# Delta rule's opening: constants and a decay exponential made beforehand, three DMA issues moved from ScalarE to SyncE, modulation sums moved to the rotating PSUM banks

## The chip, the cores and the metric

The kernel runs on one core of one Trainium2 chip. A core has five engines that run side by side, each with its own instruction queue worked off in order: TensorE (PE in the profile; its weight loads are shown as PEld), VectorE (DVE), ScalarE (ACT), GpSimd (POOL) and SyncE (SP), which here only issues DMAs. ScalarE can issue DMAs too; such an issue stands in ScalarE's own queue (ACTq), one of SyncE in SPq. TensorE writes its products to PSUM, which has eight banks; VectorE and ScalarE read them from there.

The metric is the device time of one execution in microseconds (us), as the median of several runs.

## The reference

Two layers of a diffusion backbone on 256 latent tokens, with 256 context tokens as a prefix, width 1024, all in float32. Each layer is a mixer, then a SwiGLU, each followed by a layer normalization, with shift, scale and gate ("modulation") that come from a conditioning vector. Layer 0's mixer is attention, layer 1's a chunked gated delta rule. What matters here, cut down:

```python
def reference(...):
    for i in range(DEPTH):
        mod_lat = jnp.split((silu(c) @ w_mod[i] + b_mod[i])[:, None, :], 6, axis=-1)
        u_lat = modulate(h_lat, mod_lat[0], mod_lat[1])        # the context likewise
        y_ctx, y_lat = mla_mixer(...) if i % 2 == 0 else gdn_mixer(...)
        h_lat = layer_norm(ALPHA * h_lat + mod_lat[2] * y_lat, ln1_g[i], ln1_b[i])
        f_lat = swiglu(modulate(h_lat, mod_lat[3], mod_lat[4]), w_ffn_in[i], w_ffn_out[i])
        h_lat = layer_norm(ALPHA * h_lat + mod_lat[5] * f_lat, ln2_g[i], ln2_b[i])

def gdn_project(h, w_in, conv_w, a_log, dt_bias):
    proj = h @ w_in
    qkv = short_conv(proj[..., :GDN_QKV_W], conv_w)            # 5 taps along the tokens, then silu
    q, k, v = ...                                              # q and k normalized per head
    z = proj[..., GDN_QKV_W:GDN_QKV_W + GDN_VW]
    ba = proj[..., GDN_QKV_W + GDN_VW:].reshape(B, T, 2, 2, GDN_V_HEADS)
    beta = sigmoid(ba[..., 0, :])
    g = -exp(a_log) * softplus(ba[..., 1, :] + dt_bias)        # the log decay of each step
    return q, k, v, z, beta, g

# delta rule, in chunks, forward and backward, per head:
# S_t = exp(g_t) (I - beta_t k_t k_t^T) S_{t-1} + beta_t k_t v_t^T,  o_t = S_t^T q_t
```

## The kernel before

Activations lie with the features on the 128 partitions, in eight blocks, and the tokens (256 context, 256 latent) along the free axis. Weights are streamed from HBM in tiles; ScalarE rounds each to a reduced type (`whi`, L185) and VectorE takes the rest (`wlo`, L186), and a product of float32 quality is three matmuls (`mm3`, L213 to L215). The order on each engine is not written out by hand: a planner lays out the instructions by priority, mostly that of the program's order, with a model of their times, so an instruction can stand before or behind others of the program; `after(x)` keeps instructions behind `x` on its engine. Once laid out, each engine works its queue in order.

PSUM is handed out by tags. `bank(name, tag)` takes a bank of the tag given. In layer 0's second half (`psB`) seven banks rotate under the tag `bank` and one stands alone under `md`. In the delta rule (`psC`) the same eight are divided anew: two `pj`, one `tp`, two `inv`, two `ch`, one `av`. A bank of the new division can be written once the last reader of the old tile in it is done.

The modulation is made in chunks (`Chunks`, L309 and on): a chunk `(layer, part)` has eight rows of 512 KB, each four matmuls into one PSUM tile (`modps`, L347; the profile shows two records for each), then a copy by ScalarE (`modsb`, L351), a fold by TensorE (L354) and an addition by VectorE (L356), which ends the use of the bank. `mods_in` says which pool, buffers and PSUM tag the chunks use from there on.

Around the change the program goes thus:

- `swiglu_wide` ends layer 0. Its output blocks (`ffo`) are joined to `h`; each block is squared by ScalarE (L414) for the variance, and the sums go to TensorE (`lnstat`, L424).
- Chunks (1,2) and (1,3) come next, with rows as half tiles `raw` in eleven buffers and with the one `md` bank. `normalize` makes mean and factor (`rs_y`, L244 to L248) and spreads them over a bank each (`lnbc`, L476).
- `make_uh` normalizes `h` (L513, L514), modulates it (`uw`, L517) and splits it into `uhi` (L518) and `ulo` (L519). Behind the last split ScalarE writes the layer's `h` (L522), and its queue issues the store of `h` to DRAM (`hl_dram`, L1470).
- Three `head` products take three banks of `bank` (L1474): the 64 rows for `beta` and `g`, and the first two key blocks.
- `gdn` begins. ScalarE issues the loads of a mask (`cmask`, L839) and of matrices for sums (`gsum`, L860). VectorE makes `cw` (half the taps, L841), `gn` (L843) and `eye` (L846). The first head is copied (L861), turned by TensorE (`batp`, L864), and a chain of small operations makes `beta` and `g` from it (L874 to L916); in it ScalarE makes `al`, the exponential of `a_log` (L893), and VectorE changes its sign (L894).
- Then the steps of `GDN_STEPS`. `keys0` convolves the two key heads (`conv`: a copy with a factor by ScalarE, L943, four taps by VectorE, L946, then tanh, L947, and L949). `queries0`, `values0`, `keys1` and so on project first (`product`) into a bank that `proj_bank` picks, from `pj` and `ch` in turn, and convolve it. `base` makes a decay matrix of a group and eliminates it on GpSimd (L1057, L1058, then L1077 and L1078 in turn); `decays` masks its own on GpSimd (L1134); `invert` uses the eliminated matrices on TensorE (`T`, L1192).

Of the kernel before, what the change touches and what calls it, by code (L numbers as in the profile page):

```python
# [9 lines left out]
F32 = mybir.dt.float32  # L10
F32R = mybir.dt.float32r
I32 = mybir.dt.int32
AF = mybir.ActivationFunctionType
ALU = mybir.AluOpType
AX = mybir.AxisListType.X
PSUM = bass.MemoryType.PSUM

P = 128
D = 1024
NB = D // P  # L20
TS = 256
T = 2 * TS
# [12 lines left out]
def _take(n):  # L35
    global _off
    o = _off
    _off += n
    return o
# [7 lines left out]
PC_CONV = _take(160)  # L47
PC_GN = _take(1)
PC_DT = _take(32)
PC_AL = _take(32)  # L50
# [14 lines left out]
GC_CMASK = _take(64)  # L65
# [31 lines left out]
def tile_trunk(ctx: ExitStack, tc: tile.TileContext, xT, params, consts, gconsts, wmod, w0, w1, out):  # L97
    nc = tc.nc
    V, S, G, PE = nc.vector, nc.scalar, nc.gpsimd, nc.tensor

    cp = ctx.enter_context(tc.tile_pool(name="cp", bufs=1))
# [4 lines left out]
    def open_pool(st, name, bufs=1, **kw):  # L106
        return st.enter_context(tc.tile_pool(name=name, bufs=bufs, reuse_waits="tile", **kw))
# [5 lines left out]
    def bank(name="bank", tag="bank"):  # L113
        tags = env["tags"]
        if tag not in tags:
            tag = next(t for t in ("bank", "ch", "pj") if t in tags)
        return env["ps"].tile([P, 512], F32, name=name, tag=tag, bufs=tags[tag])


    def after(ins):  # L120
        return nullcontext() if ins is None else tc.issue_after(ins.ins)


    par = cp.tile([P, NPAR], F32, name="par")
    nc.scalar.dma_start(out=par, in_=params)
    ident = cp.tile([P, P], F32, name="ident")
# [150 lines left out]
    S.activation(sc, craw, AF.Tanh, scale=0.5)  # L277
    V.scalar_tensor_tensor(sc, sc, 1.0, craw, op0=ALU.add, op1=ALU.mult)
    V.tensor_scalar(cst[:, :, 0:2], sc.rearrange("p (k s) -> p k s", s=2), 0.5, None, op0=ALU.mult)
    modv = [cp.tile([P, 48, 2], F32, name=f"modv{l}") for l in range(2)]  # L280

    def mod_part(l, js, i):
# [77 lines left out]
    def chunks(*lc):  # L360
        return [(l, c, k) for l, c in lc for k in range(8)]

    def mods_in(pool, bufs, bufs2=1, tag="md", rows="mraw"):
        env["mraw"] = (pool, rows, bufs, "modsb", bufs2, tag)

    def flush_mods():
        env["mods"].step(96)


    def mod(l, c):  # L370
        return modv[l][:, 8 * c:8 * c + 8]

    def lnp(l, i):
        o = PC_LN + l * 32 + i * 8
        return par[:, o:o + 8]

    def tok(s):
        return slice(s * TS, s * TS + TS)
# [8 lines left out]
    def ln_mod(l, g, b, lm, c_shift, c_scale):  # L387
        s1 = cp.tile([P, 8, 2], F32, name="ln1s", tag="ln1s")
        A = cp.tile([P, 8, 2], F32, name="lnA", tag="lnA")
        B = cp.tile([P, 8, 2], F32, name="lnB", tag="lnB")  # L390
        V.tensor_scalar(s1, mod(lm, c_scale), 1.0, None, op0=ALU.add)
        V.tensor_tensor(A, s1, lnp(l, g).unsqueeze(2).to_broadcast([P, 8, 2]), op=ALU.mult)
        V.tensor_tensor(B, s1, lnp(l, b).unsqueeze(2).to_broadcast([P, 8, 2]), op=ALU.mult)
        V.tensor_tensor(B, B, mod(lm, c_shift), op=ALU.add)
        return A, B
# [11 lines left out]
    class Residual:  # L407
# [3 lines left out]

        def square(self, m):
            sq = self.pool.tile([P, self.n], F32, name="lnsq", tag="lnsq", bufs=2)
            S.activation(sq, self.r[m], AF.Square)  # L414
            return sq


# [89 lines left out]
    def make_uh(r, mb, rs, ins, A, B, u, streams, pool, l, g, b, hh, sl):  # L507
        done = [ins, ins]
        n = rs.shape[1]
        for fb in range(NB):  # L510
            if mb is not None:
                with after(done[-2]):
                    V.tensor_tensor(r[fb], r[fb], mb, op=ALU.subtract)  # L513
            done.append(V.tensor_tensor(r[fb], r[fb], rs, op=ALU.mult))  # L514
            w = pool.tile([P, n], F32, name="uw", tag="lnsq", bufs=2)
            for i, s in enumerate(streams):
                S.activation(w[:, tok(i)], r[fb][:, tok(i)], AF.Identity, scale=A[:, fb, s:s + 1], bias=B[:, fb, s:s + 1])  # L517
            hi = S.activation(u[0][:, fb, 0:n], w, AF.Copy)  # L518
            last = V.tensor_tensor(u[1][:, fb, 0:n], w, f32(u[0][:, fb, 0:n]), op=ALU.subtract)  # L519
        for fb in range(NB):  # L520
            with after(hi):
                S.activation(hh[fb], r[fb][:, sl], AF.Identity, scale=lnp(l, g)[:, fb:fb + 1], bias=lnp(l, b)[:, fb:fb + 1])  # L522
        return last

    def new_u(shape=(P, NB, T)):
        return (bp.tile(list(shape), F32R, name="uhi", tag="uhi"), bp.tile(list(shape), F32R, name="ulo", tag="ulo"))
# [304 lines left out]
    def gdn(st, u, head, pool, big, fetch_base):  # L831
# [3 lines left out]
        def tl(shape, tag, bufs=1, dt=F32):  # L835
            return pool.tile(list(shape), dt, name=tag, tag=tag, bufs=bufs)

        cmask = tl([P, 2, 32], "cmask")
        nc.scalar.dma_start(out=cmask.rearrange("p d t -> p (d t)"), in_=gconsts[:, GC_CMASK:GC_CMASK + 64])  # L839
        cw = tl([P, 5, 32], "cw")  # L840
        V.tensor_scalar(cw.rearrange("p a b -> p (a b)"), par[:, PC_CONV:PC_CONV + 160], 0.5, None, op0=ALU.mult)  # L841
        gn = tl([P, 1], "gn")
        V.tensor_scalar(gn, par[:, PC_GN:PC_GN + 1], 0.5, None, op0=ALU.mult)  # L843
        XA = [tl([P, 8, 64], f"XA{i}") for i in range(2)]
        eye = tl([P, 32], "eye")
        V.reduce_sum(eye, ident.rearrange("p (b i) -> p i b", b=4), axis=AX)  # L846


        b1, b2, b3 = big(), big(), big()
        gsum, bavt = b1[:, 0:6 * P], b1[:, 6 * P:8 * P]  # L850
        bsb, gT = b2[:, 0:T], b2[:, T:T + P]

        def col(t):
            return t.rearrange("p (d u c e) -> p d u c e", d=2, u=8, c=4)
# [2 lines left out]
        yv, e, s_, q_ = (b3[:, i * 2 * P:i * 2 * P + 2 * P] for i in range(4))  # L857
        s2 = b2[:, T + P:T + 3 * P]
        beta, gcc, ngc, egc, edec, egl, neg = (col(tl([P, P], n)) for n in ("beta", "gcc", "ngc", "egc", "edec", "egl", "neg"))
        nc.scalar.dma_start(out=gsum, in_=gconsts[:, 0:6 * P])  # L860
        S.activation(bsb[0:64], head[0][0:64], AF.Copy)  # L861
        tp = bank("batp", "tp")
        for c in range(4):
# [25 lines left out]
        V.scalar_tensor_tensor(q_, q_, 1.0, s_, op0=ALU.add, op1=ALU.mult)  # L889
        V.tensor_scalar(q_, q_, 2.0, None, op0=ALU.mult)  # L890
        V.scalar_tensor_tensor(q_, yv, 0.0, q_, op0=ALU.max, op1=ALU.add)
        al = b2[:, T + 3 * P:T + 3 * P + 32]
        S.activation(al, par[:, PC_AL:PC_AL + 32], AF.Exp)  # L893
        V.tensor_scalar(al, al, -1.0, None, op0=ALU.mult)  # L894
        for d in range(2):
            V.tensor_tensor(col(e[:, 0:P])[:, d], col(q_[:, 0:P])[:, d], rows(al, d), op=ALU.mult)
        gs = bank("gsums", "inv")
# [473 lines left out]
    i = FFN0_AT  # L1371
# [17 lines left out]
    with tc.tile_pool(name="xin", bufs=1, reuse_waits="tile") as xp:  # L1389
# [4 lines left out]
        for f in range(0, NB, 2):  # L1394
# [3 lines left out]
            for fb in (f, f + 1):  # L1398
                for s in range(2):
                    a, b = A[:, fb, s:s + 1], mod(0, 0)[:, fb, s:s + 1]  # L1400
# [19 lines left out]
    wq = open_pool(l0, "wq", 8)  # L1420
    hp = open_pool(l0, "hp0")
    ln = open_pool(l0, "ln0")
    h = hp.tile([P, NB, T], F32, name="h")
    nc.sync.dma_start(out=h, in_=xT)
    g = gate(0, 2)
    res = Residual(Blocks(rp.tile([P, NB, T], F32, name="r", tag="r")), T, ln, Blocks(h))
    op = parts(o)
    env["ffn"] = dict(wp=wq, raw=11, halves=True)
    for m in range(NB):
        p = bank("mo")  # L1430
# [13 lines left out]
    res = Residual(Blocks(h), T, ln, Blocks(h))  # L1444
# [14 lines left out]
    with tc.tile_pool(name="ffn0", bufs=1, reuse_waits="tile") as pool:  # L1459
        swiglu_wide(st0, ops, res, pool, rp, finish)  # L1460
    flush_mods()
    A, B = ln_mod(0, 2, 3, 1, 0, 1)
    u = new_u()
    mods_in(wq, 5, 1, "md", "raw")
    env["mods"] = Chunks(chunks((1, 2), (1, 3)))
    mb, rs, ins = res.normalize()
    flush_mods()
    hl = dr.tile([P, NB, TS], F32, name="hl_dram")
    make_uh(res.r, mb, rs, ins, A, B, u, (0, 1), ln, 0, 2, 3, Blocks(h[:, :, 0:TS]), tok(1))
    nc.scalar.dma_start(out=hl, in_=h[:, :, 0:TS])  # L1470


    env["wp"], env["ahead"], env["raw"], env["halves"] = wp1[0], 6, 2, False
# [8 lines left out]
    def big():  # L1482
        return np_.tile([P, 1024], F32, name="N", tag="N", bufs=NBUF)

    def latent():
        return Blocks(*(big().rearrange("p (m t) -> p m t", m=4) for _ in range(2)))
# [6 lines left out]
    with tc.tile_pool(name="gdn", bufs=1, reuse_waits="tile") as pool:  # L1493
        last = gdn(st1, u, head, pool, big, fetch_base)
        g = gate(1, 2)
        A, B = ln_mod(1, 0, 1, 1, 3, 4)
        res = Centred(latent(), TS, pool, env["base"], latent())
        env["lntags"] = ("av", "ch")
        last(lambda m, p: res.add(p, g, m, (1,)))
        mb, rs, ins = res.normalize()  # L1500
    rp = open_pool(l1, "rp1")
    u = new_u()
    h = latent()
# [8 lines left out]
    res = Residual(latent(), TS, rp, h)  # L1512
# [187 lines left out]
```

## Time and profile before

| | us |
|---|---|
| median of 3 runs | 1451.16 (1449.6 to 1451.61) |
| the profiled execution | 1448.43 |
| its span, first to last instruction | 1446.6 |
| PE, PEld busy | 1355.4, 1169.0 |
| DVE, ACT, POOL busy | 981.6, 742.9, 220.5 |

In the rows of a timeline stand: start, duration, engine, line, operation, output and inputs, shapes and how many were merged; in square brackets the time that the engine was idle before, and what ended it. In a table of waits: who waited for whom, microseconds in total, how often, the longest. The names are the program's; tiles that share a buffer have one name, so `bsb`, `bavt`, `gsum`, `al` and the other parts of the three `big()` tiles are all called `N`. Matmuls are pipelined and their ends modelled, so their durations overlap. Busy time does not tell what an engine is worth at a place; the wait that ends last there does.

### The profile page before, as it was taken

How to read it: one execution, taken by the hardware profiler on the slowest of the kernel's cores; microseconds unless marked ns; L12 is line 12 of the kernel's file. 1: busy time of each engine (PE TensorE's matmuls, PEld its weight loads, DVE VectorE, ACT ScalarE, POOL GpSimd, SP SyncE). 2: the span in 40 equal slices, each digit the busy share in tenths (PEclk: the TensorE clock that was granted, in tenths of full speed). 3: DMA queues.
4: the chain of work that ended last, by engine and by line, in shares of the span. 5: the costliest groups of instructions: out<-in, count | busy, mean ns of one | idle time of the engine just before them, and what ended most of it. 6: DMA issues, size and time to landing. Idle time of an engine off the chain costs nothing.

```text
span 1446.6 us, 27846 instructions
## 1 busy us (share of the span) xinstructions
PE 1355.4 (94%) x10753; PEld 1169.0 (81%) x10753; DVE 981.6 (68%) x2038; ACT 742.9 (51%) x1611; POOL 220.5 (15%) x329
## 2 busy tenths in 40 slices
PE   7999999999999999999798879898997998999996
PEld 4767687768989998987587768787886897899996
DVE  3355566869856865867699977678676656556665
ACT  3434444356634552552648546576576543755542
POOL 0000000040000000000007984925510000000000
PEclk9979999999999999999999889899999998999998
DMA  9444412665431332255247455354243243555651
GB/s 380 146 143 150 131 44 89 239 235 174 129 119 63 114 129 76 88 184 195 78 110 211 135 139 135 104 138 122 87 129 114 86 138 131 188 187 180 187 178 59
DMA packets 131692, 204.75 MB, mean 142 GB/s; under 512 B 70632, under 2 KB 72040, under 8 KB 131432
## 3 DMA queue, kind: packets, MB, share of 16 engines
q1 hardware_dynamic: 129656, 200.90, 43.6%
q10 hardware_dynamic: 1904, 2.08, 0.5%
q8 instruction: 84, 1.38, 0.4%
q14 instruction: 48, 0.39, 0.1%
HBM read 192.92 MB, written 10.03 MB: 140 GB/s over the span
## 4 chain that ended last, share of the span: by engine, by line
PE 74%; ACT 6%; DVE 5%; POOL 5%; DMA 5%; issue 4%; SPq 1%; ACTq 0%; POOLq 0%; DVEq 0%
PE ffo L214 4%; PE ffo L215 4%; PE ffo L213 4%; PE x L213 3%; PE x L214 3%; PE x L215 3%; PE modps L347 3%; POOL mt L1077 2%; POOL m L1078 2%; PE pw L1256 2%; DMA mraw<-in_wmod_dram 1%; PE pg L213 1%; PE y L213 1%; PE y L215 1%; PE y L214 1%
## 5 line engine op out<-in xcount | busy, mean ns | idle before, releaser
L186 DVE TENSOR_TENSOR wlo<-raw,whi 128x512 fp32r<-128x512 f32 x422 | 297.4, 711 | 204.9 <-ACT whi L185 185.8
L185 ACT ACTIVATE whi<-raw 128x512 fp32r<-128x512 f32 x422 | 262.8, 630 | 304.4 <-PE ffo L214 77.9
L214 PE MATMUL ffo<-hidl,whi 128*128 128x512 f32 (+1 forms) x352 | 119.2, 339 | 0.1
L215 PE MATMUL ffo<-hidh,wlo 128*128 128x512 f32 (+1 forms) x352 | 119.1, 338 | 0.0
L213 PE MATMUL ffo<-hidh,whi 128*128 128x512 f32 (+1 forms) x352 | 118.7, 341 | 0.0
L185 ACT ACTIVATE whi<-wsum 128x512 fp32r<-128x512 f32 x88 | 55.1, 631 | 60.9 <-PE x L214 26.7
L1077 POOL TENSOR_TENSOR mt<-m 128x31 f32<-128x31 f32 (+15 forms) x124 | 77.4, 625 | 9.0
L1078 POOL TENSOR_TENSOR m<-m,mt 128x31 f32<-128x31 f32 (+15 forms) x124 | 75.1, 606 | 9.2
L214 PEld LDWEIGHTS ffo<-hidl,whi 128*128 128x128 f32 x352 | 66.8, 190 | 8.2 <-DVE hidl L219 0.6
L213 PEld LDWEIGHTS ffo<-hidh,whi 128*128 128x128 f32 x352 | 66.7, 190 | 7.9 <-ACT hidh L218 0.4
L215 PEld LDWEIGHTS ffo<-hidh,wlo 128*128 128x128 f32 x352 | 66.8, 190 | 7.7
L186 DVE TENSOR_TENSOR wlo<-wsum,whi 128x512 fp32r<-128x512 f32 x88 | 59.8, 686 | 16.5 <-ACT whi L185 16.2
L213 PE MATMUL z<-uhi,whi 128*128 128x256 f32 x216 | 64.1, 297 | 5.4 <-DVE rs_t L246 5.3
L214 PE MATMUL z<-ulo,whi 128*128 128x256 f32 x216 | 64.6, 299 | 0.3 <-DVE ulo L553 0.3
L215 PE MATMUL z<-uhi,wlo 128*128 128x256 f32 x216 | 63.4, 293 | 0.0
L1168 POOL MEMSET XA<- 128x512 f32 x2 | 1.0, 526 | 363.4 <-DMA raw<-in_wmod_dram 363.4
L213 PE MATMUL v<-uhi,whi 128*128 128x512 f32 x128 | 52.8, 413 | 1.4 <-ACT whi L185 1.4
L1521 POOL TENSOR_TENSOR N<-N,mean 128x256 f32<-128x256 f32 x4 | 2.8, 722 | 336.4 <-DVE rs_t L247 336.4
L214 PE MATMUL v<-ulo,whi 128*128 128x512 f32 x128 | 53.1, 415 | 0.0
L560 POOL TENSOR_TENSOR r<-r,rstd 128x512 f32<-128x512 f32 x4 | 6.3, 1588 | 303.3 <-ACT rstd L549 302.6
L215 PE MATMUL v<-uhi,wlo 128*128 128x512 f32 x128 | 52.0, 407 | 0.0
L347 PE MATMUL modps<-mraw,cst 128*32 128x256 f32 x512 | 47.1, 427 | 3.7 <-DMA mraw<-in_wmod_dram 3.5
(473 smaller groups left out, 4294.8 us busy)
## 6 DMA issues: line engine op xcount, KB each, us to landing
raw<-in_w_dram SPq DMA_DIRECT2D x153, 512.0 KB, 3.6
mraw<-in_wmod_dram SPq DMA_DIRECT2D x80, 512.0 KB, 4.7
raw<-in_w_dram SPq DMA_DIRECT2D x138, 256.0 KB, 2.9
raw<-in_wmod_dram SPq DMA_DIRECT2D x32, 256.0 KB, 4.1
N<-g_dram SPq DMA_DIRECT2D x16, 512.0 KB, 4.2
x<-in_xT_dram SPq DMA_DIRECT2D x4, 512.0 KB, 10.2
h<-in_xT_dram SPq DMA_DIRECT2D x1, 2048.0 KB, 8.7
m<-g_dram SPq DMA_DIRECT2D x16, 128.0 KB, 4.7
```

What stands on the lines that cost most here:

```text
L185: S.activation(hi, src, AF.Copy)
L186: V.tensor_tensor(lo, src, f32(hi), op=ALU.subtract)
L213: PE.matmul(ps_ap, a[0], b[0], start=first, stop=False, **kw)
L214: PE.matmul(ps_ap, a[0], b[1], start=False, stop=False, **kw)
L215: return PE.matmul(ps_ap, a[1], b[0], start=False, stop=last, **kw)
L347: PE.matmul(p[32 * b:32 * b + 32, 0:TS], cst[:, k], w[b], start=k == 0, stop=k == 7, tile_position=(0, 32 * b))
L560: (V if fb < 4 else G).tensor_tensor(r[fb], r[fb], rs if fb == 0 else f, op=ALU.mult)
L1077: G.tensor_tensor(tv, m[:, 0:j, j:j + 1].to_broadcast([P, j, w]), m[:, j:j + 1, j:32].to_broadcast([P, j, w]), op=ALU.mult)
L1078: G.tensor_tensor(m[:, 0:j, j:32], m[:, 0:j, j:32], tv, op=ALU.subtract)
L1168: G.memset(X, 0.0)
L1256: PE.matmul(pw[:, e_ * P:e_ * P + P], N[d][:, 2 * c + e_], rr[:, e_], start=True, stop=True)
L1521: G.tensor_tensor(res.r[fb], res.r[fb], ms, op=ALU.subtract)
```

## The change

`cw`, `gn`, `eye` and a tile of its own for `al` are made in the constants' pool; the first three right after the conditioning vector at the kernel's start. The exponential of `a_log` and its sign change are issued in layer 0's end, the exponential behind the last square of `h` on ScalarE. The store of `h` and the loads of `cmask` and `gsum` are issued by SyncE. The chunks (1,2) and (1,3) take their PSUM tiles from the seven rotating banks, not from `md`.

```diff
@@ after the conditioning vector
+    cw, gn, eye, al = (cp.tile(x, F32, name=n) for n, x in (("cw", [P, 5, 32]), ("gn", [P, 1]), ("eye", [P, 32]), ("al", [P, 32])))
+    V.tensor_scalar(cw.rearrange("p a b -> p (a b)"), par[:, PC_CONV:PC_CONV + 160], 0.5, None, op0=ALU.mult)
+    V.tensor_scalar(gn, par[:, PC_GN:PC_GN + 1], 0.5, None, op0=ALU.mult)
+    V.reduce_sum(eye, ident.rearrange("p (b i) -> p i b", b=4), axis=AX)
@@ Residual.square
-            S.activation(sq, self.r[m], AF.Square)
+            self.squared = S.activation(sq, self.r[m], AF.Square)
@@ gdn
-        nc.scalar.dma_start(out=cmask.rearrange("p d t -> p (d t)"), in_=gconsts[:, GC_CMASK:GC_CMASK + 64])
-        cw = tl([P, 5, 32], "cw")
-        V.tensor_scalar(cw.rearrange("p a b -> p (a b)"), par[:, PC_CONV:PC_CONV + 160], 0.5, None, op0=ALU.mult)
-        gn = tl([P, 1], "gn")
-        V.tensor_scalar(gn, par[:, PC_GN:PC_GN + 1], 0.5, None, op0=ALU.mult)
+        nc.sync.dma_start(out=cmask.rearrange("p d t -> p (d t)"), in_=gconsts[:, GC_CMASK:GC_CMASK + 64])
-        eye = tl([P, 32], "eye")
-        V.reduce_sum(eye, ident.rearrange("p (b i) -> p i b", b=4), axis=AX)
...
-        nc.scalar.dma_start(out=gsum, in_=gconsts[:, 0:6 * P])
+        nc.sync.dma_start(out=gsum, in_=gconsts[:, 0:6 * P])
...
-        al = b2[:, T + 3 * P:T + 3 * P + 32]
-        S.activation(al, par[:, PC_AL:PC_AL + 32], AF.Exp)
-        V.tensor_scalar(al, al, -1.0, None, op0=ALU.mult)
@@ tile_trunk, between the layers
     flush_mods()
+    with after(res.squared):
+        S.activation(al, par[:, PC_AL:PC_AL + 32], AF.Exp)
+    V.tensor_scalar(al, al, -1.0, None, op0=ALU.mult)
     A, B = ln_mod(0, 2, 3, 1, 0, 1)
     u = new_u()
-    mods_in(wq, 5, 1, "md", "raw")
+    mods_in(wq, 5, 1, "bank", "raw")
     env["mods"] = Chunks(chunks((1, 2), (1, 3)))
...
-    nc.scalar.dma_start(out=hl, in_=h[:, :, 0:TS])
+    nc.sync.dma_start(out=hl, in_=h[:, :, 0:TS])
```

## The prediction, made before the result was seen

> **What bounds the kernel now.** I read the page first, for the chain of waits, then the busy time by stage around the start of the delta rule (columns: stretch, its length, then busy us of TensorE, its weight loads, VectorE, ScalarE, GpSimd; TensorE clock; DMA share; GB/s).
>
> ```profile
> PE 74%; ACT 6%; DVE 5%; POOL 5%; DMA 5%; issue 4%; SPq 1%; ACTq 0%; POOLq 0%; DVEq 0%
> ```
>
> ```profile
> 685.00:695.00 10.00, 8.30 (x80) 4.08 (x79) 7.16 (x17) 3.13 (x7) 0.99 (x2) 0.93 0.44 138
> ...
> 712.00:720.20 8.20, 0.46 (x4) 0.34 (x5) 5.47 (x12) 3.40 (x6) 0.00 (x0) 0.82 0.57 175
> 720.20:730.00 9.80, 9.78 (x58) 9.39 (x59) 9.60 (x22) 5.89 (x13) 0.00 (x0) 0.80 0.13 37
> 730.00:740.00 10.00, 10.00 (x47) 8.13 (x46) 10.00 (x26) 3.92 (x8) 0.00 (x0) 1.00 0.41 122
> 740.00:750.00 10.00, 10.00 (x56) 8.46 (x55) 8.40 (x15) 5.26 (x12) 0.00 (x0) 1.00 0.22 63
> 750.00:760.00 10.00, 10.00 (x130) 9.04 (x129) 8.68 (x20) 4.21 (x7) 0.41 (x1) 1.00 0.78 184
> ```
>
> TensorE carries the chain, so only its holes and what stretches it count. One hole stands in the change's place: of 712.0 to 720.2 TensorE works 0.46 us. After it TensorE is full to 760, and VectorE nearly so. The table of waits says what the hole waits for:
>
> ```profile
> PE q L213 <- DVE acc L946: 7.0, 1, 7.0
> ```
>
> The first query projection waits for the convolution that reads `head`: its bank is one of theirs. The timelines of ScalarE and VectorE show why that convolution is late:
>
> ```profile
> 710.62 0.59 ACTq L1470 DMA_DIRECT2D hl_dram<-h  x1
> 711.25 0.67 ACTq L860 DMA_DIRECT2D N<-in_gconsts_dram  x1
> 712.09 0.59 ACT L861 ACTIVATE N<-head 64x512 f32<-64x512 f32 x1 [1.50 <-PE head L215]
> ...
> 712.70 1.28 ACT L893 ACT_TABLE_LOAD   x1
> 713.99 0.23 ACT L893 ACTIVATE N<-par 128x32 f32<-128x32 f32 x1
> 714.68 1.27 ACT L943 ACTIVATE acc<-head,cw 128x512 f32<-128x512 f32 x2 [0.46 <-DVE gn L843]
> ```
>
> ```profile
> 714.25 0.18 DVE L894 TENSOR_SCALAR N<-N 128x32 f32<-128x32 f32 x1 [6.89 <-ACT N L893]
> 714.35 0.24 DVE L841 TENSOR_SCALAR cw<-par 128x160 f32<-128x160 f32 x1
> 714.50 0.15 DVE L843 TENSOR_SCALAR gn<-par 128x1 f32<-128x1 f32 x1
> 714.56 0.36 DVE L846 TENSOR_REDUCE eye<-ident 128x32 f32<-128x128 f32 x1
> 715.40 5.33 DVE L946 SCALAR_TENSOR_TENSOR acc<-head,cw,acc 128x510 f32<-128x510 f32 x8 [0.48 <-ACT acc L943]
> ```
>
> `cw`, which the convolution needs, stands on VectorE behind the sign change of `al`, which waits 6.89 us for ScalarE's exponential, which stands behind a table load, behind two DMA issues.
>
> The other place is the normalization before `head`. First TensorE's timeline, then ScalarE's, then VectorE's:
>
> ```profile
> 677.61 1.05 PE L424 MATMUL lnstat<-o_mean,lnsum 128*128 128x1 f32 x8
> ...
> 685.44 2.85 PE L347 MATMUL modps<-raw,cst 128*32 128x256 f32 x36
> 688.22 1.16 PE L476 MATMUL lnbc<-i_eighth,rs_y 128*128 128x128 f32 x8
> 689.31 1.49 PE L347 MATMUL modps<-raw,cst 128*32 128x256 f32 x16
> 691.90 1.94 PE L347 MATMUL modps<-raw,cst 128*32 128x256 f32 x12 [1.10 <-DMA raw<-in_wmod_dram]
> ...
> 694.90 0.97 PE L213 MATMUL head<-uhi,whi 128*128 128x512 f32 x3
> ```
>
> ```profile
> 674.60 0.63 ACT L414 ACTIVATE lnsq<-h 128x512 f32<-128x512 f32 x1 [2.19 <-DVE lnsqs L451]
> ```
>
> ```profile
> 690.20 2.07 ACT L517 ACTIVATE uw<-h,lnB,lnA 128x256 f32<-128x256 f32 x4 [12.09 <-DVE h L514]
> 693.94 0.38 ACT L351 ACTIVATE modsb<-modps 128x256 f32<-128x256 f32 x1 [1.67 <-PE modps L347]
> ```
>
> ```profile
> 683.71 0.17 DVE L356 TENSOR_TENSOR modv<-modps,par 128x16 f32<-128x16 f32 x1 [0.57 <-PE modps L354]
> ...
> 685.98 0.16 DVE L248 SCALAR_TENSOR_TENSOR rs_y<-rs_t,rs_y 128x4 f32<-128x4 f32 x1
> ```
>
> The second modulation chunk, (1,3), starts only at 685.44, after the first gave back the one `md` bank (L356, 683.71). So 36 of its records stand ahead of the spread of `rs_y`, which is ready at 686.14 and starts at 688.22; the last twelve wait for their rows, and ScalarE's copy of them waits 1.67 us ahead of the split that `head` needs.
>
> **The change part by part.** The sum is made against the profiled execution: 1448.43 us, of which the span is 1446.6. The runs' median is 1451.16, 2.73 above it; I carry the difference over.
>
> *Constants, exponential, issues.* The convolution's ScalarE copy no longer waits for table load, `al`, `cw`, `gn`. It can follow the copy of `head` (712.09 + 0.59 = 712.68) instead of starting at 714.68: 2.0 us. Without the issues in front that copy itself can start earlier, by no more than the 0.67 us of the second issue; the wait on `head` may hide that. So 2.0 to 2.7; I take 2.3, since the table puts 1.50 us of its wait down to the last `head` matmul. This shift holds for VectorE, which is nearly full afterwards, so I pass all of it on. Where the parts go: table load and exponential, 1.51 us, stand behind the last square (674.60 + 0.63), where ScalarE has little to do until 690.20 (12.09 us idle); without that cover they would cost 1.51. The sign change, 0.18, goes beside lnstat, and the three constants, 0.75 us, to the kernel's start, where VectorE waits 5.41 us for the first weights (uncovered: 0.75):
>
> ```profile
> 12.46 0.69 DVE L186 TENSOR_TENSOR wlo<-raw,whi 128x512 fp32r<-128x512 f32 x1 [5.41 <-ACT whi L185]
> ```
>
> The store of `h` and the two loads go to SP, whose queue is quiet there:
>
> ```profile
> 659.25 29.53 SPq L325 DMA_DIRECT2D raw<-in_wmod_dram  x24
> 727.68 21.22 SPq L142 DMA_DIRECT2D raw<-in_w_dram  x5
> ```
>
> The store of `h` waits on SP for the last write of `h`; behind it stand the mask, the sums' matrix and, from 727.68 on, the weights. None is issued in the gap: nothing. Were weights pulled into it, the store's wait would cost them up to its own 0.59 us issue.
>
> *Head banks.* Where the three `head` banks come to lie is decided by the order in which banks are given back, and two more allocations before them move it. If the first projections' banks are then free, TensorE gains at most 7.0 us, and what its slow start costs:
>
> ```profile
> 720.00:724.00 4.00, 3.78 (x18) 3.81 (x19) 3.83 (x12) 3.22 (x8) 0.00 (x0) 0.50 0.00 0
> 724.00:728.00 4.00, 4.00 (x34) 3.96 (x34) 3.97 (x7) 1.90 (x5) 0.00 (x0) 0.99 0.00 0
> ```
>
> After the hole the granted clock is 0.50 for 4 us: some 2.0 us lost. But VectorE drains the banks, and it is late next. From 720.2 to 760 it idles 0.20 + 0 + 1.60 + 1.32 = 3.12 us. So beyond the 2.3 the banks are worth 0 to 3.1, not 9; I take 1.7, about half, since some of these idles are round trips to ScalarE.
>
> *Modulation banks.* The chunk (1,3) may start as its rows land. From above: the spread starts 2.08 us earlier (688.22 to 686.14), and the wait and copy of `modsb`, 1.67 + 0.38, go: 4.1. From below: its 64 records are TensorE work (2.85 + 1.49 + some 0.8 for twelve, about 5 us) that may land ahead of lnstat at 677.61 instead, which is on the chain too: minus 5.1 + 4.1 = minus 1.0, or worse by rows that they then wait for (1.10 in the row of 691.90). I take 2.0, half of the upper end: most rows of (1,3) cannot have landed at 677, since their buffers are those of the first chunk, so few records can go ahead, and some still stand in front of the spread. The two chunks now hold two of the seven banks that `ffo` uses, of which three are begun ahead and one more is filled at a time: five are enough, no wait.
>
> Sum: 2.3 + 1.7 + 2.0 = 6.0; 1448.4 − 6.0 = 1442.4, as a median 1445.2. What is late next is the decay chain on GpSimd:
>
> ```profile
> 759.60 2.37 POOL L1057 TENSOR_TENSOR m<-m,cmask 128x1024 f32<-128x1024 f32 x1 [66.01 <-DVE wlo L186]
> ...
> 783.26 2.40 POOL L1057 TENSOR_TENSOR m<-m,cmask 128x1024 f32<-128x1024 f32 x1
> ...
> 786.51 2.39 POOL L1058 TENSOR_TENSOR m<-m,ngc 128x1024 f32<-128x1024 f32 x1
> 788.86 1.67 POOL L1134 TENSOR_SCALAR_AFFINE_SELECT N<-N 128x512 f32<-128x512 f32 x2
> ...
> 790.93 1.68 POOL L1134 TENSOR_SCALAR_AFFINE_SELECT N<-N 128x512 f32<-128x512 f32 x2
> ```
>
> It begins with the decays that VectorE makes from `head`, so it moves with VectorE.
>
> **Rivals.** *Banks miss:* `head` still lies under one of the first projections. Then 2.3 + 2.0 remain: 1446.9. For it: nothing in the change names a bank. Against: the rotation does move by two. Chance 0.10.
>
> *Cold start:* once the records of (1,3) are gone from in front of `head`, TensorE has nothing between the spread's end (688.22 + 1.16 = 689.38) and `head` (694.90): 5.5 less the 2.05 saved is a hole of 3.5 us. The hole of 7.0 was followed by half the clock and 2.0 us lost; the stage with the hole of 1.10 still shows 0.93. With 2.0 lost, 4.0 remain: 1447.2. Against: some records will still stand there. The Trainium skill, "TensorE: Matmul & The Clock Gate", Part 1, speaks for this rival and so against the change: an idle window of about 3.4 us halves the clock, until about 3.4 us of work have passed. No run here shows a hole of that size. Chance 0.12.
>
> *Given back:* an earlier start makes the planner order the delta stage anew, and waits behind it eat the gain, as VectorE's full 730 to 740 suggests for the banks' part; about 1 us remains: 1450. Against: GpSimd and VectorE start earlier with the same work. Chance 0.19.
>
> *Slower:* on GpSimd the second group's mask, decay and selects cut into the first group's elimination: 2.40 + 2.39 + 1.67 + 1.68 = 8.1 us. If the new order lets one more such packet go first, the elimination ends 8.1 later. With 4.3 won (banks as little as in the first rival) that is 3.8 slower: 1455.0. It decides where the packet costs 2.9 more than is won: over 7.2 with 4.3 won; with the whole 6.0 it would end at 1453.3, within the bound. For it: the first query's data then come before the elimination. Against: the packet's order follows data that all move alike. Chance 0.16.
>
> **How the numbers follow.** Forecast 0.43, rivals in their order 0.10, 0.12, 0.19, 0.16. The measurement tells about 0.2%, 2.9 us, from no change: faster is below 1448.3, slower above 1454.1. Faster: 0.43 + 0.10 + 0.12 = 0.65, less 0.03 for the near edge of the two rivals: 0.62. Same 0.22, slower 0.16. The forecast's own range is 1441.3 (2.7 + 3.1 + 4.1 = 9.9) to 1450.2 (2.0 + 0 − 1.0). Adding the given-back case and the nearer part of the slower one, and a few us below for a better order: 1439.5 to 1454.
>
> **What would show it.** Right: no wait of the first `q` on L946, TensorE's hole at the opening under 2 us with a clock near 1.0 after it, the first L946 about 1.3 us after the copy of `head` starts instead of 3.3 (715.40 − 712.09), `head` starting about 2 us sooner after the last `ffo`, no table load behind `head`. Wrong: `q` or `batp` waiting for L946, modulation records ahead of lnstat with DMA waits, `head` at half clock, or a GpSimd elimination interrupted more than before.

## The result, and the profile after

The change made the kernel slower: 1459.17 us median against 1451.07 for the kernel before in the same set, ratio 1.0051, 95% interval [1.0028, 1.0075]. A second set gave 1458.78 against 1453.42, ratio 1.0043 [1.0022, 1.0064]. The profile of the first set is of a disturbed execution (2598.34 us, in which TensorE was busy 2555.2 us with the same 10753 records that take 1355.4 before), so everything below is read from the second set's, 1458.46 us, span 1456.7.

In it, lines of the delta rule stand 4 lower than before (the taps L946 are L942, ScalarE's factor copy L943 is L939, the copy of `head` L861 is L860) and those of the layer's parts 5 higher (`modps` L347 is L352, `modsb` L351 is L356).

The page's chain of waits, which carried the first argument, is of no use here: its shares sum to 28%, so the chain could not be followed further back.

```profile
PE 21%; issue 3%; DVE 2%; ACT 1%; DMA 1%; POOL 0%; ACTq 0%; SPq 0%; POOLq 0%; DVEq 0%
```

So I cut both kernels at the same events, each by the start of a matmul: layer 0's last `ffo`, the first `head`, the last `head`, the first `q`. Busy time by stage, the kernel before (stretch, length, busy us of TensorE, weight loads, VectorE, ScalarE, GpSimd, clock, DMA share, GB/s):

```profile
672.70:694.90 22.20, 19.84 (x175) 13.09 (x173) 11.18 (x32) 4.05 (x9) 0.99 (x2) 0.85 0.64 214
694.90:711.40 16.50, 16.50 (x73) 13.27 (x72) 9.25 (x18) 14.33 (x27) 0.00 (x0) 1.00 0.00 1
711.40:720.20 8.80, 0.82 (x6) 0.34 (x5) 5.47 (x12) 3.40 (x6) 0.00 (x0) 0.83 0.54 168
```

The changed kernel:

```profile
670.10:695.00 24.90, 18.12 (x118) 11.71 (x116) 15.41 (x37) 6.96 (x13) 0.00 (x0) 0.72 0.33 106
695.00:722.80 27.80, 27.80 (x141) 16.70 (x140) 5.52 (x13) 12.91 (x26) 0.98 (x2) 0.94 0.46 158
722.80:724.90 2.10, 0.85 (x7) 0.37 (x5) 1.62 (x3) 1.61 (x3) 0.00 (x0) 1.00 0.00 0
```

The hole in front of the first `q` is gone: 8.80 us became 2.10. But `head` starts 2.7 us later after `ffo` (24.90 against 22.20) and takes 27.80 us instead of 16.50, with 141 matmul records in it instead of 73. Before, next to no DMA traffic fell into that stage (1 GB/s); now 158 GB/s do. TensorE's timeline of the changed kernel says what came in:

```profile
672.79 1.02 PE L429 MATMUL lnstat<-o_mean,lnsum 128*128 128x1 f32 x8 [2.26 <-DVE lnsum L455]
...
681.35 2.05 PE L481 MATMUL lnbc<-i_eighth,rs_y 128*128 128x128 f32 x8 [0.59 <-DVE rs_y L248]
683.33 3.34 PE L352 MATMUL modps<-raw,cst 128*32 128x256 f32 x44
687.46 0.63 PE L352 MATMUL modps<-raw,cst 128*32 128x256 f32 x4 [0.80 <-DMA raw<-in_wmod_dram]
689.13 0.62 PE L352 MATMUL modps<-raw,cst 128*32 128x256 f32 x4 [1.05 <-DMA raw<-in_wmod_dram]
...
695.05 0.80 PE L213 MATMUL head<-uhi,whi 128*128 128x512 f32 x1
...
704.04 0.40 PE L213 MATMUL head<-uhi,whi 128*128 128x512 f32 x1
704.27 0.39 PE L214 MATMUL head<-ulo,whi 128*128 128x512 f32 x1
704.59 0.63 PE L352 MATMUL modps<-raw,cst 128*32 128x256 f32 x4
705.15 0.51 PE L215 MATMUL head<-uhi,wlo 128*128 128x512 f32 x1
```

Before, all 64 records of chunk (1,2) stood ahead of `lnstat`, and (1,3) stood around `lnbc` (the prediction's rows at 685.44 to 691.90). Now no record of either stands ahead of `lnbc`: (1,2) begins at 683.33, behind the last spread, and all but four records of (1,3) are strewn in fours and eights between the `head` products. Two neighbouring `head` products start 0.23 us apart (704.04, 704.27); with four records between them it is 0.88 (704.27, 705.15), 0.65 more.

What the records wait for stands in the table of waits of that stretch (672 to 726), and why the rows are late in SyncE's own timeline and its own table of waits (640 to 710):

```profile
PE modps L352 <- DMA raw<-in_wmod_dram: 3.7, 5, 1.0
```

```profile
656.72 46.96 SPq L330 DMA_DIRECT2D raw<-in_wmod_dram  x27
```

```profile
SPq L330 <- PE modps L352: 24.2, 5, 17.4
```

The loads of the rows take SyncE's queue from 656.72 to 703.68, where they took 29.53 us for 24 before. A load needs one of the eleven `raw` buffers; with (1,2) unsummed until 683, none comes back (one of SyncE's waits for the sums is 17.4 us long), and the rows of (1,3) come that much later. ScalarE's timeline shows the price ahead of `head`: its queue works in order, and the copy of the sums stands in front of the split that `head` needs.

```profile
672.73 1.28 ACT L1459 ACT_TABLE_LOAD   x1
674.02 0.23 ACT L1459 ACTIVATE al<-par 128x32 f32<-128x32 f32 x1
684.22 2.08 ACT L522 ACTIVATE uw<-h,lnB,lnA 128x256 f32<-128x256 f32 x4 [9.97 <-DVE h L519]
...
694.39 0.38 ACT L356 ACTIVATE modsb<-modps 128x256 f32<-128x256 f32 x1 [4.35 <-PE modps L352]
694.67 0.62 ACT L523 ACTIVATE uhi<-uw 128x512 fp32r<-128x512 f32 x1
...
715.27 0.39 ACT L356 ACTIVATE modsb<-modps 128x256 f32<-128x256 f32 x1 [6.33 <-PE modps L352]
722.56 1.38 ACT L939 ACTIVATE acc<-head,cw 128x512 f32<-128x512 f32 x2 [6.91 <-PE head L215]
```

### The profile page after: what moved, and what is told of

Its sections match the earlier page's. It is cut to its first block, busy times and chain, and to the rows that moved or that the text cites. A ratio compares the mean times of both kernels' runs of the same rounds, so it can differ in the third digit from the quotient of the medians.

```text
span 2596.6 us, 27850 instructions
## 1 busy us (share of the span) xinstructions
PE 2555.2 (98%) x10753; PEld 2051.1 (79%) x10753; DVE 990.1 (38%) x2038; ACT 756.4 (29%) x1611; POOL 206.7 (8%) x329
## 3 DMA queue, kind: packets, MB, share of 16 engines
q1 hardware_dynamic: 130984, 202.38, 24.6%
## 4 chain that ended last, share of the span: by engine, by line
PE 97%; DVE 1%; ACT 1%; DMA 0%; issue 0%; ACTq 0%; SPq 0%; DVEq 0%
PE ffo L213 5%; PE ffo L215 5%; PE ffo L214 5%; PE modps L352 3%; PE x L213 3%; PE x L214 3%; PE x L215 3%; PE v L214 3%; PE v L213 3%; PE v L215 3%; PE pw L1252 2%; PE z L213 2%; PE z L214 2%; PE z L215 2%; PE ks L1244 2%; PE pw L1258 2%
## 5 line engine op out<-in xcount | busy, mean ns | idle before, releaser
L213 PE MATMUL ffo<-hidh,whi 128*128 128x512 f32 (+1 forms) x352 | 195.9, 562 | 0.0
L215 PE MATMUL ffo<-hidh,wlo 128*128 128x512 f32 (+1 forms) x352 | 195.6, 556 | 0.0
L214 PE MATMUL ffo<-hidl,whi 128*128 128x512 f32 (+1 forms) x352 | 195.3, 555 | 0.0
L213 PEld LDWEIGHTS ffo<-hidh,whi 128*128 128x128 f32 x352 | 115.7, 329 | 29.9 <-issue 27.7
L214 PEld LDWEIGHTS ffo<-hidl,whi 128*128 128x128 f32 x352 | 115.1, 327 | 27.9 <-issue 25.4
L215 PEld LDWEIGHTS ffo<-hidh,wlo 128*128 128x128 f32 x352 | 113.8, 323 | 29.0 <-issue 26.6
L213 PEld LDWEIGHTS z<-uhi,whi 128*128 128x128 f32 x216 | 74.1, 343 | 4.6 <-issue 2.8
L214 PEld LDWEIGHTS z<-ulo,whi 128*128 128x128 f32 x216 | 74.8, 346 | 3.2 <-issue 2.3
L213 PE MATMUL x<-t,whi 128*128 128x256 f32 x176 | 77.1, 438 | 0.0
L214 PE MATMUL x<-t,whi 128*128 128x256 f32 x176 | 77.1, 438 | 0.0
L215 PEld LDWEIGHTS z<-uhi,wlo 128*128 128x128 f32 x216 | 76.1, 352 | 0.6 <-issue 0.4
```

The costliest lines, as they stand in the source:

```text
L213: PE.matmul(ps_ap, a[0], b[0], start=first, stop=False, **kw)
L214: PE.matmul(ps_ap, a[0], b[1], start=False, stop=False, **kw)
L215: return PE.matmul(ps_ap, a[1], b[0], start=False, stop=last, **kw)
```

## The experiments

Each but e8, a single run of 1451.44 us, was timed against the kernel before in the same set. Stage lengths are taken between the starts of matmuls in each profile: **A** from the last `ffo` to the last of `batp`, **B** from there to the first `q`, **C** from the first tap on VectorE (`acc<-head`) to `gsums`, **D** from the first `T` to the next SwiGLU's first product. "const" are the constants and the exponential made early, "issues" the three DMA issues on SyncE, "rotation" the chunks on the tag `bank`. A profile is one execution: those of e2, e12 and e5 are 8.5, 7.4 and 6.4 us under their kernels' medians, that of e6 2.6 over, so the stages, D above all, are good to some microseconds only.

| run | what is in it | ratio to before | A | B | C | D |
|---|---|---|---|---|---|---|
| before | | 1 | 40.3 | 7.2 | 26.6 | 391.2 |
| e8 | nothing, second profile | | 39.7 | 7.2 | 27.5 | 394.0 |
| e6 | const | 0.9973 [0.9954, 0.9993] | 39.7 | 5.7 | 26.2 | 392.2 |
| e12 | const, once more | 0.999 [0.997, 1.001] | 39.7 | 5.7 | 25.9 | 388.4 |
| e5 | issues | 1.0 [0.9978, 1.0021] | 38.5 | 7.1 | 31.2 | 384.9 |
| e7 | const, head banks | 1.0034 [1.0018, 1.0051] | 40.2 | 0.2 | 25.8 | 397.5 |
| e2 | const, issues | 1.0038 [1.0015, 1.006] | 39.0 | 5.0 | 30.4 | 394.4 |
| e4 | const, issues, other tags | 1.0006 [0.999, 1.0022] | 38.9 | 5.0 | 30.3 | 393.6 |
| e3 | rotation | 1.0066 [1.0042, 1.009] | 52.8 | 0.1 | 24.6 | 392.5 |
| e10 | const, rotation | 1.0114 [1.0084, 1.0143] | 49.7 | 0.2 | 24.0 | 397.0 |
| e1 | const, issues, rotation: the change | 1.0043 [1.0022, 1.0064] | 54.6 | 0.2 | 25.9 | 386.9 |
| e9 | const, two md banks | 1.0064 [1.0039, 1.0088] | 47.6 | 0.2 | 31.5 | 397.4 |
| e11 | const, issues, two md banks | 0.9995 [0.9973, 1.0017] | 47.9 | 0.3 | 30.1 | 385.7 |

### Undoing the rotation (e1 to e3)

e1 is the changed kernel; e2 leaves the chunks on `md`; e3 is the kernel before with the rotation alone:

```diff
-    mods_in(wq, 5, 1, "md", "raw")
+    mods_in(wq, 5, 1, "bank", "raw")
```

Expected of e1:

> The changed kernel itself, for a profile of an undisturbed execution. Theory A (modulation): both chunks, 128 records of TensorE, now stand behind the normalization's spread and between the head products, because a tile that takes its place in the rotation of the seven banks cannot be filled before the tiles that come ahead of it in the program; the stage from the last ffo to batp is some 8 to 12 us longer than before's 40 us, the opening behind it some 3 to 5 us shorter: ratio 1.003 to 1.007. Theory B (opening): the layer norm's stage is as long as before and the delta stage behind it, ordered anew, is longer by 7 us.

Of e2:

> The changed kernel with the modulation chunks on the md bank again; constants, exponential and DMA issues stay moved. Theory A: before less 2.3 us of the opening, about 0.998 of before; the first q waits for L946-like taps again, some 5 us instead of 7.0. Theory B: as slow as the change, 1.005.

Of e3:

> The kernel before with only the modulation chunks on the rotating banks. Theory A: the change without the constants' gain, so 2 to 3 us slower than the change: 1.006 to 1.009 of before. Theory B: the modulation is innocent: before or a little faster, 0.996 to 1.0.

Stage A parts them: 54.6 and 52.8 us with the rotation, 39.0 without. That is the loss of the opening, and it needs nothing else of the change. But e2 is not faster than e1 in the time (1.0038 against 1.0043, where 0.998 was expected), though its stage A is 15.6 us shorter. So something else takes time in e2, behind the opening: its `gsums` come 30.4 us after the first tap instead of 26.6, and D is 394.4 against 386.9. These stages do not show all of it, since the profiled execution is the fastest of e2's twelve.

### Other banks for head by the tags (e4)

e4 is e2 with the list of `head` products swapped in front of `linears` and the tags of the first projections in the order `pj, ch, ch, pj, ch`, meant to free the first `q`.

> As the run with md, and the head products kept off the first projections' banks in another way: the first two head products exchange their banks, and the first projections take ch, ch, pj in place of ch, pj, ch. By theory A this has the gain of the banks without the late modulation: another 0 to 3 us below the run with md, about 1446, and no wait of the first q for the convolution. If VectorE alone sets the pace it equals the run with md within 1 us. Theory B: as slow as the change or slower.

The edit missed: a bank is given out at a tile's first write, and the order of the writes was as before. The first `q` still waits for the taps, as the table of waits of e4 (669 to 745) shows:

```profile
PE q L213 <- DVE acc L942: 4.8, 1, 4.8
```

What it does show is the wait with the constants and the issues moved: 4.8 us instead of 7.0. Its time is 4.5 us under e2's (1454.09, 1458.57) with the opening the same; what makes that difference is open.

### Issues alone, constants alone (e5, e6, e12), and the kernel before again (e8)

e5 has only the three issues moved to SyncE; e6 only `cw`, `gn`, `eye` and the exponential of `a_log` made early, as in the change's diff; e12 is e6 again.

> The kernel before with only the three DMA issues (store of h, loads of cmask and gsum) moved from ScalarE to SyncE. In the built order this alone moves gsums on TensorE behind some 15 more k matmuls. Theory A (the moved issues are what ate the gain of the constants in e2_md, where gsums came 30.6 us after batp's end against 29.0, and T to pw took 27.0 against 20.5): 2 to 6 us slower than before, gsums at least 1.5 us later after batp, T to pw near 27. Theory B (the prediction's 'nothing'): within 1 us of before, and T to pw is 20 to 27 from run to run whatever the order.

> The kernel before with only the constants made at the start and the exponential of a_log behind the last square; the issues stay on ScalarE, the chunks on md. TensorE's order is that of before. Theory A (the prediction's step on constants was right by itself and was eaten by the moved issues): conv's first ScalarE copy straight behind the copy of head, first q 2 us earlier after batp's end than before (5.0 to 5.4 instead of 7.2), gsums about 2 us earlier, total 1.5 to 2.5 us faster. Theory B (what is won at the opening is lost behind it whatever the order, since the delta stage waits for something else): first q earlier, but total within 0.7 us of before.

> The kernel before, unchanged, for a second profile of it. If stage lengths differ from kernel to kernel by their order, the second profile repeats the first: batp's end to the first q 7.2 us, to gsums 29.0, T to pw 20.5. If T to pw differs from run to run, it comes out several us away from 20.5, up to the 27 of the other kernels.

> e6_constants_only once more, as the base of this batch and to see whether its gain repeats. With TensorE's order unchanged and the opening 1.5 to 2.3 us shorter: ratio to before 0.9975 to 0.999, and batp's end to the first q 5.5 us. If the first measurement was luck: 0.999 to 1.001.

The second profile of the kernel before repeats its stages within 1 us at the opening, and D within 2.8. Constants alone are the one part that helps: 0.9973 and 0.999; 3.9 and 1.5 us by the ratios, though the second interval reaches over 1. From the last of `batp` to `gsums` the two take 27.1 and 26.8 us, the two profiles of before 29.0 and 29.9. The order of TensorE's matmuls from `batp` on is that of the kernel before, down to the last, so this is the clean measurement of the step. ScalarE and VectorE in e6:

```profile
713.14 0.59 ACT L860 ACTIVATE N<-head 64x512 f32<-64x512 f32 x1 [1.50 <-PE head L215]
...
714.18 1.27 ACT L939 ACTIVATE acc<-head,cw 128x512 f32<-128x512 f32 x2 [0.45 <-issue]
```

```profile
714.90 5.33 DVE L942 SCALAR_TENSOR_TENSOR acc<-head,cw,acc 128x510 f32<-128x510 f32 x8 [6.47 <-ACT acc L939]
...
722.33 0.95 DVE L878 RECIPROCAL beta<-beta 128x128 f32<-128x128 f32 x1
...
727.27 0.48 DVE L942 SCALAR_TENSOR_TENSOR acc<-q,cw,acc 128x255 f32<-128x255 f32 x1
...
737.68 0.34 DVE L892 TENSOR_TENSOR N<-N,al 128x64 f32<-128x64 f32 x2
```

The taps start 1.76 us after the copy of `head` starts (714.90 − 713.14), not 3.31. Of the 0.45 us in front of L939 the row says only "issue", the issue of the mask's load standing there. In e5 that is gone: its taps start 2.8 us after the start of the last `head` (710.99 − 708.2) against 4.0 before (715.40 − 711.4) and 2.4 in e6 (714.90 − 712.5); with both, in e2, 0.7 (708.10 − 707.4). So the issues are worth 1.2 to 1.7 at this place, more than the 0.67 that I allowed. But e5 is no faster. Its `gsums` come 31.2 us behind the first tap, 4.6 later than before, because the planner, which now has the loads on SyncE, lays TensorE's order anew: between `batp` and `gsums` stand 11 matmuls of `k` before, 29 in e5 and 25 in e2. They start 0.23 us apart, so the 18 more of e5 are about 4.1 us. Late weights are not seen to be the reason: in TensorE's waits from 705 to 860 neither e5 nor e2 has one for a weight load.

### The head banks by themselves (e7)

e6 with the rows of the weights for `head` and the list permuted, so that the first key block lies in bank 1 and the beta rows in the bank of the first `q`:

```diff
-        L += [beta_rows(wi, k), _blk(wi, k, 8), _blk(wi, k, 9)]
+        L += [_blk(wi, k, 8), beta_rows(wi, k), _blk(wi, k, 9)]
...
     linears(st1, head, parts(u))
+    head[0], head[1] = head[1], head[0]
...
-            return bank(name, ("pj", "ch", "pj", "ch", "ch")[early[0] % 5] if early[2] else "pj")
+            return bank(name, ("pj", "ch", "ch", "pj", "ch")[early[0] % 5] if early[2] else "pj")
```

(`beta_rows` stands for the padded slice of 64 columns.)

> e6_constants_only with the head banks freed for the first projections: the rows of the head weights and the list are permuted so that the beta rows lie in the bank of the first key block and the first key block in bank 1, and the second projection takes a ch bank. TensorE's order is otherwise that of before. The first q then needs only the bank that ScalarE's copy of head gives back. Theory A (the head banks are worth something by themselves): no wait of q for acc L946, first q within 1 us of batp's end, gsums 3 to 5 us earlier after batp than in the kernel before, total 3 to 6 us faster than before. Theory B (VectorE drains the banks and is what is late): first q early, gsums no earlier than in e6_constants_only, total as e6_constants_only.

It does what it says. TensorE's row of the first `q` in e6, and then in e7, where it starts 0.2 us after `batp`:

```profile
719.73 0.55 PE L213 MATMUL q<-uhi,whi 128*128 128x256 f32 x1 [5.48 <-DVE acc L942]
```

```profile
713.49 0.39 PE L213 MATMUL q<-uhi,whi 128*128 128x256 f32 x1
```

And it is worth nothing. VectorE's timeline in e7:

```profile
714.22 5.33 DVE L942 SCALAR_TENSOR_TENSOR acc<-head,cw,acc 128x510 f32<-128x510 f32 x8 [6.47 <-ACT acc L939]
...
721.65 0.95 DVE L878 RECIPROCAL beta<-beta 128x128 f32<-128x128 f32 x1
...
726.59 0.48 DVE L942 SCALAR_TENSOR_TENSOR acc<-q,cw,acc 128x255 f32<-128x255 f32 x1
...
736.99 0.35 DVE L892 TENSOR_TENSOR N<-N,al 128x64 f32<-128x64 f32 x2
```

Beside e6's rows every instruction stands 0.68 or 0.69 us earlier, which is what `batp` itself is earlier (713.10 against 713.79): the first taps of `q`, whose product was there 6 us sooner, too. VectorE works through the same queue almost without a pause (in e6 it is busy 24.90 of the 25.10 us to 740), so what TensorE hands it sooner lies and waits; the table of waits of e7 (711 to 745) shows that TensorE gets its time back as a wait for VectorE:

```profile
PE k L215 <- DVE wlo L186: 2.9, 1, 2.9
```

Behind this wait the clock falls to half as it did behind the hole, only later (0.50 from 728.25 to 735.08). Up to the first `T` the two are level: 126.7 us from `batp` in e7, 126.5 in e6.

The slowdown, 9 us against e6 in the same set (1456.99, 1447.71), comes later, in D. From the 378th matmul record behind `batp` on TensorE's order differs from e6's, and in the stretch from `batp` to the next SwiGLU products of the recurrence wait longer for ScalarE. That says where the time goes, not why. First e6's row, then e7's:

```profile
PE pw L1258 <- ACT w L1254: 2.9, 3, 1.5
```

```profile
PE pw L1258 <- ACT w L1254: 7.7, 4, 3.7
PE pw L1252 <- ACT w L1254: 4.2, 1, 4.2
```

### A second bank for the modulation outside the rotation (e9, e11), and the rotation with the constants (e10)

e9 is e6, and e11 the changed kernel, with two banks under `md` and six that rotate; e10 is e6 with the rotation.

```diff
-    open_psum(pb_, "psB", bank=7, md=1)
+    open_psum(pb_, "psB", bank=6, md=2)
```

> e6_constants_only with the eight banks of psB divided into six rotating and two under md, so that both modulation chunks have a bank of their own and none waits in the rotation. In the built order the first records of (1,3) stand among lnstat, and all of (1,2) before it. Theory A (the change's modulation step failed because the chunks were put into the rotation, behind the statistics): last ffo to batp's end at most 40 us, as in e6_constants_only (39.7), down to 37.6 if the 2.1 us of the prediction's modulation step are there; total within 3 us of e6_constants_only, or better. Theory B (the modulation records cost about 14 us wherever a second bank is given to them, for instance because they crowd TensorE or their rows are late): about 50 us or more for that stage, total 6 us or more above e6_constants_only.

> e6_constants_only with the chunks in the rotation: the changed kernel without its three moved DMA issues. TensorE's order up to batp is that of the changed kernel. Theory A (chunks in the rotation are the loss): last ffo to batp's end 52 to 55 us, total 6 to 12 us above e6_constants_only, about that of the changed kernel (ratio to before 1.003 to 1.008). Theory B (the moved issues, with the rest, are the loss): stage 52 to 55 us all the same, but total within 3 us of e6_constants_only.

> The changed kernel, with its chunks in two md banks (six rotate) instead of in the rotation. Theory A: the opening as in e9_two_md; 5 to 10 us faster than the changed kernel. Whether it beats e9_two_md depends only on the order that the planner gives to the delta stage: 3 us either way. Theory B: as the changed kernel, 1.004 of before.

e10 confirms the rotation's price a third time: A is 49.7 instead of e6's 39.7, the time 1.0114 of before. That is 18 us over e12 of the same set (1467.91, 1449.62), more than the 6 to 12 expected and more than stage A explains; the rest lies behind the opening (D 397.0 against 388.4). In e9 and e11 the modulation records no longer stand in `head`; TensorE in e9:

```profile
682.23 2.78 PE L352 MATMUL modps<-raw,cst 128*32 128x256 f32 x20
684.94 2.08 PE L481 MATMUL lnbc<-ident,lnmean 128*128 128x128 f32 x8
686.94 1.44 PE L352 MATMUL modps<-raw,cst 128*32 128x256 f32 x16
688.31 1.16 PE L481 MATMUL lnbc<-i_eighth,rs_y 128*128 128x128 f32 x8
...
693.21 0.98 PE L213 MATMUL head<-uhi,whi 128*128 128x512 f32 x3
...
718.76 0.66 PE L863 MATMUL batp<-ident,N 64*128 64x64 f32 x4 [6.42 <-ACT th L943]
```

`head` starts 21.7 us after the last `ffo` (693.21 − 671.5), which is e6's and e12's 21.5 and 21.7: (1,3), which starts 10.7 us after that `ffo` (682.23) instead of 12.7 (685.44 − 672.7), gains nothing there by its earlier start. The stage was still 47.6 us, not the 40 that theory A gave, and for a reason that neither theory had: with six banks in the rotation, the bank of `batp` lies under the second key block, so that `batp` waits 6.42 us until the taps have read it. (The view names the tanh, L943, which reads no bank; the last tap ends at 718.61, 713.28 + 5.33, and `batp` starts at 718.76.) It is the hole of the first `q` in another place. And e9 and e11, alike up to here, are 8.5 us apart in the time (1459.88, 1451.37) where 3 was expected: D is 397.4 and 385.7. They differ only in the engine of three DMA issues.

## Why the prediction was wrong

**Modulation banks** is the step that failed in the opening; a second one, the moved issues, failed behind it (below). The step on the banks said that (1,3) may start as its rows land, worth 2.0, at worst −1.0. The mechanism was taken for granted: I saw the one `md` bank as the only thing that held (1,3) back and treated the seven as free. A tag's banks are handed out in the program's order, and `lnstat` and `lnbc` stand ahead of the chunks there (the call that works the chunks, `flush_mods`, comes behind `normalize`, which asks for the banks of `lnbc`): in each of the three kernels with the rotation (e1, e3, e10) no record of a chunk stands ahead of the last `lnbc`, in every one with `md` all 64 of (1,2) stand ahead even of `lnstat`. So the chunks lost the one thing that `md` had given them, the right to be worked before the statistics. The spread did come earlier, as forecast: the last `lnbc` ends 13.3 us after the last `ffo` (681.35 + 2.05 − 670.1) instead of 16.7 (688.22 + 1.16 − 672.7). These 3.4 us were lost again at once, to the sums of (1,2), the waits for rows and the copy in front of the split (−2.7 in all up to `head`), and 27.80 − 16.50 = 11.3 more in `head`. Together 14.0, and stage A shows 54.6 − 40.3 = 14.3. The prediction's own sign for this, "modulation records ahead of lnstat with DMA waits", named the wrong side of `lnstat`. Its "five are enough, no wait" counted banks, not their order.

**Constants** was right: 2.3 predicted, 2.0 of it for the constants alone; 3.9 and 1.5 measured in e6 and e12. There the taps follow the copy of `head` by 1.76 us, where I named 1.3; with the issues moved as well, in e2, by 1.20 (708.10 − 706.90). The exponential behind the last square costs nothing, as its rows at 672.73 show: ScalarE is idle for 9.97 us behind it. Within this step the **issues** were called "nothing" on SyncE, which holds for the time of e5 (1.0). It does not hold with the constants: e2 gave 1.0038 where the constants alone gave 0.9973 and 0.999. A moved issue makes the planner lay out the delta stage anew, and the prediction, which knew this only as a rival, put it at nothing here. That the new order is what costs the time is argued from the profiles, not shown by a run.

**Head banks**: the rotation did move them, and the first `q` lost its wait, as hoped. The price was 1.7 (0 to 3.1), and the lower end was right. I took about half, because some of VectorE's idle time is round trips to ScalarE; e7 says that VectorE limits wholly. In e6, e12, e7 and e1, `gsums` come 25.8 to 26.2 us behind the first tap, whether the first `q` starts 4.8 us after that tap (e6, e12) or 0.7 before it (e7: 713.5 against 714.22). e3 and e10 do it in 24.6 and 24.0, but in another order.

**The rivals.** "Banks miss" did not happen. "Cold start" did in part: the first `head` products of e1 run at half clock (below), yet not for a hole behind `lnbc`. Its reading of the 0.93 in 685 to 695 was wrong, too: the clock was 0.50 up to 686.50 and 1.00 from there on, so the hole of 1.10 at 691.90 has no part in it. "Given back" happened, though it was given 1450 and the modulation hid it: from the last of `batp` to `gsums` e1 takes 24.5 us against 29.0 and 29.9 in the two profiles of before, 4.5 to 5.4 won, and from `gsums` to the first `T` 104.3 against 98.5 and 99.5, 4.8 to 5.8 lost. "Slower" gave 1455.0 by another mechanism: from GpSimd's first mask to the first `T` e1 takes 83.7 us (769.8 to 853.5), before 80.8 (759.6 to 840.4), so no packet of 8.1 was cut in. The range ended at 1454 while the time was 1458 to 1459. With the modulation's worst end at −14.3 instead of −1.0 the range would have held it, but mending that step alone would not have made the forecast right: e2, without the rotation, is as slow.

**The sum of e1.** Up to the first `T` e1 is 15.7 us behind (853.5 − 670.1 = 183.4 against 840.4 − 672.7 = 167.7). From there to the next SwiGLU it wins 4.3 in D. By the two profiles of before, D is 391.2 and 394.0, so 4 to 7 are won back, and 9 to 11 remain between profiles, against 6.2 [3.2, 9.3] in the timed runs (0.43% of 1453.4). Nothing in the prediction foresaw these 4 to 7; without them the miss would have been larger.

**What stays open.** How the order in the delta stage sets D: it lies between 384.9 and 397.5 over thirteen profiles, and between 388.4 and 394.0 in the four with the order of before. I did not find a rule that tells a good order from a bad one, and no run pinned the order with the rest changed. The best version measured is e6, the constants alone.

## What to carry to other kernels

A pool that hands its banks out in the program's order is not free because some of its banks are: a tile that joins it is queued behind every earlier request, so work that runs ahead of the program needs a tag of its own. Before a hole on one engine is priced, look whether the engine behind it works without a pause over the same stretch; here it did, and the hole was worth nothing. Where a planner lays out the order, measure each part of a change alone and keep a version whose order is unchanged: here the same three moved issues cost nothing in e5 and 7 to 9 us in e2 (by its ratio, against e12 and e6), and e11, which has them, is 8.5 us faster than e9.

## What the runs showed of the hardware

TensorE's clock fell to half without a long hole. Busy time by stage of e1 ahead of `head`:

```profile
687.00:691.00 4.00, 1.88 (x12) 0.43 (x12) 4.00 (x8) 1.43 (x3) 0.00 (x0) 1.00 0.81 235
691.00:695.00 4.00, 2.79 (x12) 0.59 (x12) 1.50 (x3) 0.61 (x2) 0.00 (x0) 0.54 0.97 352
695.00:698.00 3.00, 3.00 (x9) 2.38 (x8) 1.98 (x3) 2.94 (x7) 0.00 (x0) 0.50 1.05 380
```

The longest hole there is 1.05 us (the row at 689.13); but TensorE was busy 1.88 of 4.00 us, and from about 691 to 698 it had half the clock. The Trainium skill, "TensorE: Matmul & The Clock Gate", Part 1, ties the half clock, in its table of the two states, to an idle window of about 3.4 us. The trace agrees for long holes: after e6's 5.48 us the clock was 0.51 for 3.8 us, and after e7's 0.98 it stayed at 1.00.

```profile
719.70:723.50 3.80, 3.77 (x18) 3.80 (x19) 3.63 (x11) 3.19 (x8) 0.00 (x0) 0.51 0.00 0
```

```profile
713.40:719.40 6.00, 6.00 (x51) 5.82 (x49) 5.18 (x8) 1.68 (x3) 0.00 (x0) 1.00 0.61 179
```

By that row of the table alone e1 would have kept its clock: here a stretch that is busy for about half, in short pieces, was enough.

A busy share near full does not say that the clock is kept, either. In the kernel before the clock was 0.50 for 6.83 us, most of them under `lnstat` (matmuls of 128x1) and `lnbc`, though the profile has TensorE busy in all of them and in 3.12 of the 3.41 us ahead:

```profile
676.26:679.67 3.41, 3.12 (x27) 2.23 (x25) 0.00 (x0) 0.38 (x1) 0.00 (x0) 1.00 0.92 291
679.67:686.50 6.83, 6.83 (x39) 6.14 (x43) 2.77 (x17) 0.00 (x0) 0.00 (x0) 0.50 0.77 283
```

The time of one and the same kernel goes with its mean granted clock: over 29 runs of the kernel before in one set the times lie between 1444.19 and 1458.35, and a straight line through them falls by 9 us for each 0.01 of mean clock. That scatter is as large as most effects here, and is why the stages of the profiles carry the argument, not the times alone; stage D scatters as well, by 5.6 us in the four profiles with one order.
